# Two transformer blocks on one core: the convolution's sum and other intermediate values move from SBUF into PSUM

## The chip, the core and the metric

One core of a Trainium2 chip runs one program that computes everything: no host arithmetic, one launch. The metric is the device time of an execution in microseconds (us). In this program TensorE (PE) multiplies matrices out of SBUF into PSUM, of which each stage allots eight banks of 512 fp32 values per partition; VectorE (DVE) and ScalarE (ACT) work on both memories, GpSimd (POOL) on SBUF alone, and SyncE (SP) starts the DMAs.

## What is computed

The input is one sequence of 512 tokens of width 1024. A first block of two layers has three branches side by side: differential attention (two softmaxes per head, subtracted), bidirectional retention with a group norm, and grouped-query attention. Each branch is projected, multiplied by a sigmoid gate and summed:

```python
branches = jnp.stack([a, r, c], axis=2)
projected = jnp.einsum('bsnw,nwd->bsnd', branches, w_branch[l])
merged = jnp.sum(gates * projected, axis=2)
h = h + jnp.einsum('bsd,de->bse', merged, w_out[l])
```

Then an MLP with a squared ReLU. A second block of two layers has a 256-token context beside the sequence; its mixer concatenates a Fourier part, eight heads of latent attention (512 queries against 768 keys) and a convolution of 31 taps over 256 channels:

```python
def conformer_conv(zg, w_dw, b_dw, ln_g, ln_b, w_pw2):
    a, g = jnp.split(zg, 2, axis=-1)
    u = a * jax.nn.sigmoid(g)
    u = lax.conv_general_dilated(u, w_dw[:, None, :], ...,
                                 feature_group_count=CONV_WIDTH) + b_dw
    u = jax.nn.silu(layer_norm(u, ln_g, ln_b))
    return u @ w_pw2
```

In the first of these two layers the mixer runs for the sequence and the context, in the second for the sequence alone.

## The kernel before

Activations lie transposed, channels on partitions and tokens along the free axis. Every fp32 operand of a matmul is split into a high part (ACT copies it to fp32r, `hi`) and a low part (DVE subtracts it, `lo`), and three products stand for one. `out_split(y)` is this pair for an intermediate value: it reads `y` twice, once on ACT and once on DVE.

The program has eight stages, each with its own PSUM tags: for each layer a mixer and then a stage with output projection and MLP. The first block's mixers are `mixer1`, the second block's `mixer2`.

Nothing is issued as the code stands. Every operation is recorded (`Sched.record`), and at a stage's end `Sched.run` (line 283) places them: a list scheduler that takes, engine by engine, the ready operation of the lowest number, gives buffers from tags such as "mm" or "t" and holds an operation back while its tag is full. All instructions are issued by one line, so in the profile everything is L489 and only tile names tell groups apart: `cu` is the padded convolution input, `h`, `t`, `r`, `e`, `z`, `w` are SBUF tags, `mm`, `sc`, `acc` PSUM ones, and `sums` holds constant matrices. `_port` (line 532) lets DVE instructions with two SBUF operands and POOL instructions exclude each other in the scheduler's bookkeeping. Where PE would have nothing for a while, the scheduler puts in filler matmuls of `sums` with itself, whose result nobody reads. Engines work in the order that results, and semaphores between them are derived from the tiles that instructions touch.

Convolution (`taps`, line 1371, run by `conv`): for each stream and each half of the channels, 25 of the 31 taps are multiply-adds on DVE, with the sum in an SBUF tile `h`; the other 6 are products, in turn on ACT and POOL (`TAPS = 'AP'`), that POOL adds up in a second tile; POOL adds both at the end. The two channel halves are stepped together (`zip_longest`), and the steps are dealt out between the blocks of attention.

Latent attention (`attend`): for 128 queries, scores against 768 keys go into one of two slots of tag "sc2" (9 matmuls of 256 columns), DVE takes the minimum, ACT the exponential with its sum, PE transposes, ACT and DVE split, PE multiplies by the values. The two slots are two tiles of two banks each.

First block: `ret_attend` multiplies scores by a decay mask into SBUF, splits them, and normalises by head; `diff_attend` makes both exponentials in SBUF; `project` gates a branch and adds it to `merged` on POOL.

Of the kernel before, what the change touches and what calls it, by code (L numbers as in the profile page):

```python
# [12 lines left out]
F32 = mybir.dt.float32  # L13
# [6 lines left out]
P = 128  # L20
# [26 lines left out]
TICK = 3  # L47
# [4 lines left out]
B2 = {"sc2": 2, "mm tr acc ms": 4}  # L52
BESIDE = 6
TAPS = 'AP'
# [473 lines left out]
def _in_psum(x):  # L528
    return isinstance(x, View) and x.buf.tag in ("mm", "tr", "acc", "ms", "sc", "sc2")
# [36 lines left out]
def kernel(  # L566
# [195 lines left out]
    def normalized(y, rs, n):  # L762

        w, rt = t32(n), psum("tr", n)
        S.activation(w.rearrange("p (a b) -> p a b", b=64), rs.unsqueeze(2).to_broadcast([P, n // 64, 64]), AF.Copy)
        transposes(rt, w, n // P)
        V.tensor_tensor(out=y, in0=y, in1=rt, op=ALU.mult)
# [155 lines left out]
    def mixer1(l, mp, u):  # L923
# [137 lines left out]
        def project(n, bo, gated=False, early=[]):  # L1061

            for m in range(KB):
# [11 lines left out]
                V.scalar_tensor_tensor(out=g, in0=g, scalar=1.0, in1=pj, op0=ALU.add, op1=ALU.mult)  # L1075
                if not gated:
                    G.tensor_tensor(out=merged[m], in0=merged[m], in1=g, op=ALU.add)
                yield
# [13 lines left out]
        def diff_attend(hd, q, k, v, bo):  # L1092
            acc = psum("acc")
            for half in range(2):
                pt = [pair(T), pair(T)]
                for j in range(2):
                    es = [sc.alloc("e") for m in range(2)]
                    r0, r1 = (softmax(scores(q, k, m, half * 2 + j), es[m]) for m in range(2))
                    V.tensor_tensor(out=r1, in0=r1, in1=neglam, op=ALU.mult)
                    S.activation(es[0], es[0], AF.Copy, scale=r0)  # L1100
                    V.scalar_tensor_tensor(out=es[0], in0=es[1], scalar=r1, in1=es[0], op0=ALU.mult, op1=ALU.add)
                    to_pt(es[0], pt, j)
# [40 lines left out]
        def ret_attend(hd, q, k, v, z, bo):  # L1143
# [5 lines left out]
            for kt in range(4):  # L1149
# [13 lines left out]
            colsum(ms, ones128, squares(xc))  # L1163
            R = rstd(ms, 1e-5)
            r = t32()
            V.scalar_tensor_tensor(out=r, in0=xc, scalar=ncol(f"gn{l}", hd), in1=R, op0=ALU.mult, op1=ALU.mult)
            V.scalar_tensor_tensor(out=r, in0=r, scalar=0.5, in1=z, op0=ALU.mult, op1=ALU.mult)
            bo.append(out_split(r))
# [15 lines left out]
        def gqa_attend(i, q, k, v, out):  # L1184
# [16 lines left out]
            normalized(y, rs, T)  # L1201
            out.append(out_split(y))
# [80 lines left out]
        for m, _ in enumerate(project(0, bd, False, early)):  # L1283
            a, b = sc.alloc("r", pin=True), sc.alloc("r", pin=True)
            S.activation(a, merged[m], AF.Copy, scale=0.5)
# [743 lines left out]
```

## Time and profile before

| | us |
|---|---|
| median of 3 runs (3465.47 to 3468.73) | 3466.51 |
| the profiled execution | 3464.11 |
| its span, first to last instruction | 3462.3 |

| engine | busy us | share |
|---|---|---|
| PE | 3366.1 | 97% |
| DVE | 2293.6 | 66% |
| ACT | 1458.9 | 42% |
| POOL | 795.3 | 23% |

The shares are means over stages that differ. By the tiles used, the first block's mixers run from the start to 556 us and from 961 to 1493 us, the second block's from 1898 to 2196 us and from 2822 to 3047 us; projections and MLPs fill the rest. A matmul's busy time includes the filler.

### The profile page before, as it was taken

Reading aid. Unit: us, or ns where it says so; the run is one execution under the profiler, and the core shown is the slowest. Engines: PE = TensorE matmul, PEld = TensorE weight load, DVE = VectorE, ACT = ScalarE, POOL = GpSimd, SP = SyncE. Lnnn points to the kernel's source line nnn. Section 1 sums busy time; section 2 is a strip of 40 time slices with the busy share of each in tenths; the row PEclk is TensorE's granted clock in tenths of the full one; section 3 lists DMA queues with packets and bytes.
Section 4 is the critical chain, followed back from the end, with each engine's and each line's share of the span. In section 5 each row is a group of like instructions: output and inputs, shape, how many; then the busy total and the mean of one; then the engine's idle time right before and its main releaser. Section 6 shows DMA issues by size and latency. Waiting matters only on the chain.

```text
span 3462.3 us, 48309 instructions
## 1 busy us (share of the span) xinstructions
PE 3366.1 (97%) x18565; PEld 2901.3 (84%) x18565; DVE 2293.6 (66%) x4092; ACT 1458.9 (42%) x2751; POOL 795.3 (23%) x710
## 2 busy tenths in 40 slices
PE   8999999999999999999999988999999998999999
PEld 8888888888888888888888876898888887888888
DVE  8888875865388788658654998564443369963334
ACT  5555444322355554443223376441221244843223
POOL 3112323111131032231112443120110235320002
PEclk9999999999999999999999999999999999999999
DMA  3222223543332212236533110223332221123332
GB/s 126 64 71 67 74 67 134 191 168 127 106 101 65 71 61 80 73 134 195 176 128 116 46 37 7 98 80 112 109 109 92 68 81 48 32 79 98 97 96 81
DMA packets 100744, 326.14 MB, mean 94 GB/s; under 512 B 11168, under 2 KB 18336, under 8 KB 100512
## 3 DMA queue, kind: packets, MB, share of 16 engines
q1 hardware_dynamic: 100512, 323.05, 29.0%
q8 instruction: 145, 2.38, 0.3%
q14 instruction: 87, 0.71, 0.1%
HBM read 313.57 MB, written 9.44 MB: 93 GB/s over the span
## 4 chain that ended last, share of the span: by engine, by line
PE 84%; DVE 10%; ACT 3%; issue 2%; POOL 1%; DMA 0%; SPq 0%; DVEq 0%; ACTq 0%; POOLq 0%
PE mm L489 78%; PE sc L489 4%; DVE r L489 3%; DVE h L489 2%; DVE s L489 2%; PE acc L489 2%; DVE t L489 1%; ACT r L489 1%; DVE w L489 1%; ACT e L489 1%; ACT t L489 0%; DMA raw<-in_win_dram 0%; ACT w L489 0%; POOL t L489 0%; POOL x L489 0%
## 5 line engine op out<-in xcount | busy, mean ns | idle before, releaser
L489 PE MATMUL mm<-r,w 128*128 128x512 f32 (+2 forms) x12044 | 2521.2, 360 | 17.7 <-DVE w L489 7.5
L489 PEld LDWEIGHTS mm<-r,w 128*128 128x128 f32 (+1 forms) x12044 | 2009.0, 189 | 347.6 <-DVE w L489 11.0
L489 DVE TENSOR_TENSOR w<-raw,w 128x1024 fp32r<-128x1024 f32 (+2 forms) x466 | 588.2, 1270 | 639.6 <-issue 327.8
L489 ACT ACTIVATE w<-raw 128x1024 fp32r<-128x1024 f32 (+1 forms) x466 | 483.5, 1047 | 1035.1 <-PE mm L489 946.8
L489 ACT ACTIVATE e<-sc,s 128x512 f32<-128x512 f32 (+2 forms) x208 | 153.4, 740 | 99.6 <-DVE s L489 94.7
L489 POOL TENSOR_TENSOR x<-t,x 128x512 fp32r<-128x512 f32 (+1 forms) x58 | 83.0, 1434 | 409.1 <-ACT x L489 397.5
L489 PE MATMUL mm<-rc,w 128*128 128x256 f32 x768 | 166.1, 281 | 0.0
L489 PEld LDWEIGHTS mm<-rc,w 128*128 128x128 f32 x768 | 139.8, 189 | 20.2
L489 DVE TENSOR_REDUCE s<-sc 128x1 f32<-128x512 f32 (+2 forms) x208 | 151.4, 741 | 7.6 <-PE sc L489 7.1
L489 POOL TENSOR_TENSOR t<-t,t 128x512 f32<-128x512 f32 (+2 forms) x70 | 89.0, 1273 | 237.5 <-DVE t L489 200.3
L489 PE MATMUL mm<-r,r 128*128 128x256 f32 (+1 forms) x588 | 118.8, 333 | 8.1 <-DVE r L489 6.8
L489 ACT ACTIVATE t<-mm 128x512 f32<-128x512 f32 (+4 forms) x126 | 68.0, 540 | 135.0 <-PE mm L489 129.9
L489 DVE SCALAR_TENSOR_TENSOR h<-cu,half,h 128x512 f32<-128x512 f32 (+1 forms) x144 | 116.4, 819 | 0.5
L489 PE MATMUL mm<-sums 128*128 128x256 f32 x757 | 107.2, 291 | 9.7 <-DVE sums L489 6.4
L489 DVE TENSOR_TENSOR r<-mm,r 128x256 fp32r<-128x256 f32 (+1 forms) x266 | 105.6, 433 | 14.3 <-ACT r L489 12.4
L489 ACT ACTIVATE r<-mm 128x256 fp32r<-128x256 f32 (+1 forms) x272 | 94.8, 401 | 44.5 <-PE mm L489 41.3
L489 PEld LDWEIGHTS mm<-sums 128*128 128x128 f32 x757 | 101.2, 198 | 13.2 <-DVE sums L489 6.6
L489 ACT ACTIVATE r<-t 128x512 fp32r<-128x512 f32 (+3 forms) x141 | 83.1, 597 | 68.8 <-DVE t L489 55.9
L489 PEld LDWEIGHTS mm<-r,r 128*128 128x128 f32 x588 | 90.8, 193 | 23.4 <-DVE r L489 8.4
L489 DVE TENSOR_TENSOR r<-t,r 128x512 fp32r<-128x512 f32 (+2 forms) x134 | 105.4, 794 | 7.5 <-ACT r L489 6.3
L489 PE MATMUL mm<-w,r 128*128 128x256 f32 x704 | 102.4, 285 | 4.9 <-DVE w L489 3.1
L489 PEld LDWEIGHTS mm<-w,r 128*128 128x128 f32 x704 | 91.5, 190 | 7.4 <-DVE w L489 3.5
(636 smaller groups left out, 4358.8 us busy)
## 6 DMA issues: line engine op xcount, KB each, us to landing
raw<-in_wm_dram SPq DMA_DIRECT2D x256, 512.0 KB, 3.5
raw<-in_win_dram SPq DMA_DIRECT2D x134, 512.0 KB, 3.6
mraw<-in_wmod_dram SPq DMA_DIRECT2D x64, 512.0 KB, 4.4
raw<-in_wmod_dram SPq DMA_DIRECT2D x32, 512.0 KB, 3.5
raw<-in_wbr_dram SPq DMA_DIRECT2D x24, 512.0 KB, 3.5
raw<-in_wout_dram SPq DMA_DIRECT2D x16, 512.0 KB, 4.0
raw<-in_wo_dram SPq DMA_DIRECT2D x16, 512.0 KB, 3.5
kept<-h SPq DMA_DIRECT2D x24, 256.0 KB, 3.2
```

What stands on the lines that cost most here:

```text
L489: getattr(self.engines[eng], name)(*[_real(x) for x in a], **{n: _real(x) for n, x in k.items()})
```

## The change

In the second block, the convolution's running sum becomes one PSUM bank of its own, tag "cv". There is one, so a sum has to be finished before the next begins: the channel halves are stepped one after the other, and `TICK` and the count of steps double to deal out the same taps. The bank is won by packing both score slots into one tile of three banks, with slots of 768 columns where they had 1024. The products of the other six taps are all ACT's, and the last addition is DVE's. `normalized` (the softmax division after attention) and `fold` (Fourier) leave their result in PSUM.

In the first block, retention's masked scores and its group norm are computed in place in PSUM, and the ACT copy ahead of the group norm goes; differential attention's second exponential overwrites its scores; and for the last branch projected (n == 0) gate and sum are computed in the projection's own bank, on DVE, and split from there.

```diff
-TICK = 3
+TICK = 6
-B2 = {"sc2": 2, "mm tr acc ms": 4}
+B2 = {"sc2": 2, "mm tr acc ms": 4, "cv": 1}
-TAPS = 'AP'
+TAPS = "A"
...
 def normalized(y, rs, n):
-        V.tensor_tensor(out=y, in0=y, in1=rt, op=ALU.mult)
+        V.tensor_tensor(out=rt, in0=y, in1=rt, op=ALU.mult)
+        return rt
...
 def project(n, bo, gated=False, early=[]):
-                V.scalar_tensor_tensor(out=g, in0=g, scalar=1.0, in1=pj, op0=ALU.add, op1=ALU.mult)
-                if not gated:
+                V.scalar_tensor_tensor(out=g if n else pj, in0=g, scalar=1.0, in1=pj, op0=ALU.add, op1=ALU.mult)
+                if n == 0:
+                    V.tensor_tensor(out=pj, in0=merged[m], in1=pj, op=ALU.add)
+                elif not gated:
                     G.tensor_tensor(out=merged[m], in0=merged[m], in1=g, op=ALU.add)
-                yield
+                yield pj
...
 def diff_attend(hd, q, k, v, bo):
-                    es = [sc.alloc("e") for m in range(2)]
-                    r0, r1 = (softmax(scores(q, k, m, half * 2 + j), es[m]) for m in range(2))
+                    e, p0 = sc.alloc("e"), scores(q, k, 0, half * 2 + j)
+                    r0 = softmax(p0, e)
+                    p1 = scores(q, k, 1, half * 2 + j)
+                    r1 = softmax(p1, p1)
...
-                    V.scalar_tensor_tensor(out=es[0], in0=es[1], scalar=r1, in1=es[0], op0=ALU.mult, op1=ALU.add)
+                    V.scalar_tensor_tensor(out=e, in0=p1, scalar=r1, in1=e, op0=ALU.mult, op1=ALU.add)
...
 def ret_attend(hd, q, k, v, z, bo):
-                w = t32()
-                V.tensor_tensor(out=w, in0=ps, in1=dt[:, 384 - kt * P:896 - kt * P], op=ALU.mult)
-                wh, wl = out_split(w)
+                V.tensor_tensor(out=ps, in0=ps, in1=dt[:, 384 - kt * P:896 - kt * P], op=ALU.mult)
+                wh, wl = out_split(ps)
...
-            r = t32()
-            S.activation(r, acc, AF.Copy)
             xc = psum("ms")
-            colsum(xc, cen128, parts(r))
+            colsum(xc, cen128, parts(acc))
...
 for m, pj in enumerate(project(0, bd, False, early)):
-            S.activation(a, merged[m], AF.Copy, scale=0.5)
-            V.scalar_tensor_tensor(out=b, in0=merged[m], scalar=0.5, in1=a.bitcast(F32), op0=ALU.mult, op1=ALU.subtract)
+            S.activation(a, pj, AF.Copy, scale=0.5)
+            V.scalar_tensor_tensor(out=b, in0=pj, scalar=0.5, in1=a.bitcast(F32), op0=ALU.mult, op1=ALU.subtract)
...
 def taps(i, b):
-            a = accs[n, b] = sc.alloc("h", n)
-            c = sc.alloc("h", n)
+            a, c = psum("cv", n), sc.alloc("h", n)
...
-            G.tensor_tensor(out=a, in0=a, in1=c, op=ALU.add)
+            accs[n, b] = sc.alloc("h", n)
+            V.tensor_tensor(out=accs[n, b], in0=c, in1=a, op=ALU.add)
...
 def fold(ps):
-            f, y = t32(TC), t32()
+            f = t32(TC)
             S.activation(f, ps[:, TC:], AF.Copy)
-            V.tensor_tensor(out=y[:, :TC], in0=ps[:, :TC], in1=f, op=ALU.add)
-            V.tensor_tensor(out=y[:, TC:], in0=ps[:, :TC], in1=f, op=ALU.subtract)
-            return out_split(y)
+            V.tensor_tensor(out=ps[:, TC:], in0=ps[:, :TC], in1=f, op=ALU.subtract)
+            V.tensor_tensor(out=ps[:, :TC], in0=ps[:, :TC], in1=f, op=ALU.add)
+            return out_split(ps)
...
 def conv():
-            yield from zip_longest(block_taps(0), block_taps(1))
+            for b in range(2):
+                yield from block_taps(b)
...
 def phase(name, shares, slots=()):
                 if tag == "sc2":
-                    sc.slots(pp, tag, n, 1024, F32)
+                    t = pp.tile([P, n * 768], F32, tag=tag, name=tag)
+                    sc.tags[tag] = Tag([t[:, i * 768:(i + 1) * 768] for i in range(n)], 0)
```

Because the scheduler reads the new operands, the order changes on all engines of the four mixers. DVE at the convolution's beginning in the second block's second layer, before (`cu` the input, `h_143` and `h_144` the two channel halves' sums, `cu_22072` the second half's input):

```order
L489 SCALAR_TENSOR_TENSOR cu_22071<-t_122,mm_22065 128x512
L489 TENSOR_TENSOR w_107<-raw_108,w_107 128x8x32
L489 TENSOR_SCALAR h_143<-cu_22071,half,vec 128x512
L489 TENSOR_TENSOR w_103<-raw_109,w_102 128x1024
L489 SCALAR_TENSOR_TENSOR h_143<-cu_22071,half,h_143 128x512 x3
L489 SCALAR_TENSOR_TENSOR cu_22072<-t_121,mm_22063 128x512
L489 SCALAR_TENSOR_TENSOR h_143<-cu_22071,half,h_143 128x512
L489 TENSOR_SCALAR h_144<-cu_22072,half,vec 128x512
L489 SCALAR_TENSOR_TENSOR h_143<-cu_22071,half,h_143 128x512
L489 SCALAR_TENSOR_TENSOR h_144<-cu_22072,half,h_144 128x512
```

and changed, with `cv` the bank:

```order
L489 SCALAR_TENSOR_TENSOR cu_22083<-t_121,mm_22076 128x512
L489 TENSOR_TENSOR w_104<-raw_108,w_104 128x8x32
L489 TENSOR_SCALAR cv_22078<-cu_22083,half,vec 128x512
L489 TENSOR_TENSOR w_105<-raw_109,w_106 128x1024
L489 SCALAR_TENSOR_TENSOR cv_22078<-cu_22083,half,cv_22078 128x512 x6
L489 SCALAR_TENSOR_TENSOR cu_22084<-t_118,mm_22074 128x512
L489 SCALAR_TENSOR_TENSOR cv_22078<-cu_22083,half,cv_22078 128x512 x5
L489 TENSOR_TENSOR t_122<-t_122,mm_22075 32x512
L489 TENSOR_TENSOR w_104<-raw_110,w_107 128x1024
L489 TENSOR_TENSOR t_120<-t_120,mm_22076 32x256
```

The two halves' sums alternated; now a single sum advances in runs of up to six here and nine elsewhere, and eleven taps stand where five stood before the next step's work (`t_122`).

PE at a group of scores of the second block's second layer, with the semaphores that each instruction waits for; `sc_22061` and `sc_22062` are the two slots, before:

```order
L489 MATMUL sc_22061<-k0h,q0l 128x256
L489 MATMUL sc_22061<-k0h,q0h 128x256
L489 MATMUL sc_22061<-k0l,q0h 128x256
L489 MATMUL sc_22061<-k0h,q0l 128x256
L489 MATMUL mm_22063<-ident,e_22068 128x128 [waits DVE_49,Activation_49]
L489 MATMUL mm_22063<-ident,e_22068 128x128 x3
L489 MATMUL sc_22062<-k0h,q0h 128x256
L489 MATMUL sc_22062<-k0l,q0h 128x256
L489 MATMUL sc_22062<-k0h,q0l 128x256
```

and changed, where both slots are `sc_22073`:

```order
L489 MATMUL mm_22074<-ident,e_22082 128x128 x2
L489 MATMUL mm_22076<-ident,e_22080 128x128 [waits DVE_49,Activation_49]
L489 MATMUL mm_22076<-ident,e_22080 128x128 x3
L489 MATMUL sc_22073<-k0h,q0h 128x256 [waits DVE_49]
L489 MATMUL sc_22073<-k0l,q0h 128x256
L489 MATMUL sc_22073<-k0h,q0l 128x256
```

The group's first matmul waited for nothing that its engine had not already seen; now it waits for DVE. Of the 80 such groups in both layers, none waited for DVE before and 25 do now.

DVE at the end of the first block's first mixer, from the fifth output tile on (`z` a gate, `h` the sum of the other branches, `r` the split), before:

```order
L489 SCALAR_TENSOR_TENSOR z_188<-z_188,mm_166 128x512
L489 TENSOR_TENSOR w_105<-raw_110,w_103 128x1024
L489 SCALAR_TENSOR_TENSOR r_72<-h_141,r_83 128x512
L489 TENSOR_TENSOR w_104<-raw_108,w_106 128x1024
L489 TENSOR_TENSOR w_107<-raw_109,w_102 128x1024
L489 SCALAR_TENSOR_TENSOR z_183<-z_183,mm_165 128x512
L489 SCALAR_TENSOR_TENSOR r_82<-h_143,r_80 128x512
```

and changed:

```order
L489 SCALAR_TENSOR_TENSOR mm_165<-z_188,mm_165 128x512
L489 TENSOR_TENSOR mm_165<-h_141,mm_165 128x512
L489 SCALAR_TENSOR_TENSOR r_80<-mm_165,r_84 128x512
L489 TENSOR_TENSOR w_102<-raw_110,w_106 128x1024
L489 TENSOR_TENSOR w_103<-raw_108,w_107 128x1024
L489 TENSOR_TENSOR w_104<-raw_109,w_105 128x1024
L489 SCALAR_TENSOR_TENSOR mm_164<-z_184,mm_164 128x512
```

The addition that POOL made stands on DVE between gate and split, and the split reads the bank. Filler matmuls number 207, 111, 59 and 106 in the four mixers before, and 215, 119, 63 and 43 now.

## Rows read from the trace of the kernel before

**Rows 1.** Page, part 1: each engine's busy us, share of span, instructions.

```profile
PE 3366.1 (97%) x18565; PEld 2901.3 (84%) x18565; DVE 2293.6 (66%) x4092; ACT 1458.9 (42%) x2751; POOL 795.3 (23%) x710
```

**Rows 2.** Stretches, from:to and length, busy us (instructions) by engine, clock, DMA.

```profile
core 0: us, PE busy (x) PEld busy (x) DVE busy (x) ACT busy (x) POOL busy (x), PEclk, DMA share, GB/s
0.00:556.00 556.00, 540.88 (x2871) 457.35 (x2872) 443.25 (x871) 284.35 (x555) 135.81 (x105) 0.99 0.25 80
...
961.00:1493.00 532.00, 522.54 (x2774) 441.76 (x2773) 429.03 (x846) 271.95 (x529) 125.61 (x87) 1.00 0.25 77
...
1898.00:2196.00 298.00, 261.14 (x1723) 230.63 (x1723) 269.35 (x576) 182.79 (x433) 123.67 (x121) 0.96 0.13 42
...
2822.00:3047.00 225.00, 203.97 (x1360) 180.89 (x1359) 209.07 (x406) 140.90 (x314) 96.91 (x82) 0.98 0.15 49
```

**Rows 3.** DVE groups, 1898 to 2196 us: count, busy us, mean ns, idle before.

```profile
L489 DVE SCALAR_TENSOR_TENSOR h<-cu,half,h 128x512 f32<-128x512 f32 x48 | 44.3, 932 | 0.3
L489 DVE TENSOR_REDUCE s<-sc 128x1 f32<-128x768 f32 x32 | 30.1, 945 | 0.8 <-PE sc L489 0.8
L489 DVE SCALAR_TENSOR_TENSOR h<-cu,half,h 128x256 f32<-128x256 f32 x48 | 25.1, 541 | 0.1
```

**Rows 4.** DVE groups, 2822 to 3047 us: the convolution's.

```profile
L489 DVE SCALAR_TENSOR_TENSOR h<-cu,half,h 128x512 f32<-128x512 f32 x48 | 47.0, 986 | 0.2
```

**Rows 5.** Single instructions near 2854 us: start, us, engine, operation, [idle before].

```profile
2853.46 0.74 DVE L489 SCALAR_TENSOR_TENSOR h<-cu,half,h 128x512 f32<-128x512 f32 x1
...
2854.84 1.35 POOL L489 TENSOR_TENSOR h<-h,t 128x512 f32<-128x512 f32 x1
2854.97 1.78 DVE L489 SCALAR_TENSOR_TENSOR h<-cu,half,h 128x512 f32<-128x512 f32 x1
```

**Rows 6.** DVE groups of the whole run, nearest in kind.

```profile
L489 DVE TENSOR_TENSOR h<-h,mm 128x512 f32<-128x512 f32 x68 | 46.3, 681 | 11.0 <-PE mm L489 10.6
...
L489 DVE SCALAR_TENSOR_TENSOR z<-z,mm 128x512 f32<-128x512 f32 x40 | 27.1, 681 | 18.4 <-ACT z L489 10.8 <-PE mm L489 7.6
...
L489 DVE SCALAR_TENSOR_TENSOR h<-mm,mod1x,h 128x512 f32<-128x512 f32 x34 | 25.3, 745 | 5.6 <-PE mm L489 5.6
...
L489 DVE SCALAR_TENSOR_TENSOR hc<-mm,mod0c,hc 128x256 f32<-128x256 f32 x40 | 19.2, 480 | 32.5 <-PE mm L489 32.4
...
L489 DVE TENSOR_TENSOR t<-t,t 128x512 f32<-128x512 f32 x26 | 17.8, 686 | 0.6
...
L489 DVE TENSOR_TENSOR h<-h,mm 128x256 f32<-128x256 f32 x24 | 9.8, 417 | 11.6 <-PE mm L489 11.2
```

**Rows 7.** Chain of waits, 1898 to 2196 us, then 2822 to 3047: share by line.

```profile
by line: PE mm L489 29.4%; DVE r L489 11.4%; issue 11.0%; PE sc L489 6.7%; DVE h L489 6.7%; ACT r L489 5.8%; DVE s L489 5.3%; ACT e L489 5.3%; DVE t L489 3.9%; POOL t L489 2.9%; DVE w L489 2.1%; POOL x L489 2.0%; ACT t L489 1.8%; POOL h L48
...
by line: PE mm L489 29.7%; DVE r L489 10.9%; DVE h L489 8.1%; issue 7.8%; DVE s L489 6.7%; ACT r L489 5.5%; ACT e L489 5.1%; PE sc L489 4.8%; DVE t L489 3.1%; DVE w L489 2.9%; ACT t L489 2.3%; POOL x L489 1.7%; DVE k0h L489 1.2%; POOL h L48
```

**Rows 8.** ACT groups, 1898 to 2196 us: products of other taps.

```profile
L489 ACT ACTIVATE t<-cu,half 128x512 f32<-128x512 f32 x4 | 2.7, 711 | 0.0
L489 ACT ACTIVATE t<-cu,half 128x256 f32<-128x256 f32 x4 | 2.0, 505 | 0.0
```

**Rows 9.** Waits, 1898 to 2196 us: us in total, times, longest.

```profile
PE sc L489 <- ACT e L489: 7.1, 8, 1.8
...
DVE s L489 <- PE sc L489: 0.8, 1, 0.8
```

**Rows 10.** Single instructions at the end of the first mixer.

```profile
547.91 1.29 POOL L489 TENSOR_TENSOR h<-h,z 128x512 f32<-128x512 f32 x1 [6.61 <-DVE z L489]
549.24 0.63 ACT L489 ACTIVATE r<-h 128x512 fp32r<-128x512 f32 x1 [2.19 <-POOL h L489]
549.90 0.69 DVE L489 SCALAR_TENSOR_TENSOR r<-h,r 128x512 fp32r<-128x512 f32 x1 [2.13 <-ACT r L489]
```

**Rows 11.** PE group, 2822 to 3047 us: filler matmuls.

```profile
L489 PE MATMUL mm<-sums 128*128 128x256 f32 x109 | 15.1, 283 | 0.0
```

More of the change, by code (lines that the diff above doesn't have):

```diff
@@ L528, in _in_psum @@
 def _in_psum(x):
-    return isinstance(x, View) and x.buf.tag in ("mm", "tr", "acc", "ms", "sc", "sc2")
+    return isinstance(x, View) and x.buf.tag in ("mm", "tr", "acc", "ms", "sc", "sc2", "cv")
 def _port(eng, name, out, ins):
@@ L1096, in diff_attend @@
                 for j in range(2):
-                    es = [sc.alloc("e") for m in range(2)]
-                    r0, r1 = (softmax(scores(q, k, m, half * 2 + j), es[m]) for m in range(2))
+                    e, p0 = sc.alloc("e"), scores(q, k, 0, half * 2 + j)
+                    r0 = softmax(p0, e)
+                    p1 = scores(q, k, 1, half * 2 + j)
+                    r1 = softmax(p1, p1)
                     V.tensor_tensor(out=r1, in0=r1, in1=neglam, op=ALU.mult)
-                    S.activation(es[0], es[0], AF.Copy, scale=r0)
-                    V.scalar_tensor_tensor(out=es[0], in0=es[1], scalar=r1, in1=es[0], op0=ALU.mult, op1=ALU.add)
-                    to_pt(es[0], pt, j)
+                    S.activation(e, e, AF.Copy, scale=r0)
+                    V.scalar_tensor_tensor(out=e, in0=p1, scalar=r1, in1=e, op0=ALU.mult, op1=ALU.add)
+                    to_pt(e, pt, j)
                     if j:
@@ L1152, in ret_attend @@
                 mm3(ps, k[0][:, a], k[1][:, a], q[0], q[1], True, True)
-                w = t32()
-                V.tensor_tensor(out=w, in0=ps, in1=dt[:, 384 - kt * P:896 - kt * P], op=ALU.mult)
-                wh, wl = out_split(w)
+                V.tensor_tensor(out=ps, in0=ps, in1=dt[:, 384 - kt * P:896 - kt * P], op=ALU.mult)
+                wh, wl = out_split(ps)
                 mm3(acc, v[0][:, a], v[1][:, a], wh, wl, kt == 0, kt == 3)
                 yield
-            r = t32()
-            S.activation(r, acc, AF.Copy)
             xc = psum("ms")
-            colsum(xc, cen128, parts(r))
+            colsum(xc, cen128, parts(acc))
             ms = psum("acc2")
             colsum(ms, ones128, squares(xc))
+            V.scalar_tensor_tensor(out=xc, in0=xc, scalar=0.5, in1=z, op0=ALU.mult, op1=ALU.mult)
             R = rstd(ms, 1e-5)
[L1165 to L1168, printed above, removed]
+            V.scalar_tensor_tensor(out=xc, in0=xc, scalar=ncol(f"gn{l}", hd), in1=R, op0=ALU.mult, op1=ALU.mult)
+            bo.append(out_split(xc))
         def group_values():
@@ L1200, in gqa_attend @@
                 V.tensor_tensor(out=y[r], in0=y[r], in1=acc[r], op=ALU.add)
-            normalized(y, rs, T)
-            out.append(out_split(y))
+            out.append(out_split(normalized(y, rs, T)))
         got, bg, br, bd = {}, [], [], []
@@ L1282, in mixer1 @@
         mh, ml = [], []
-        for m, _ in enumerate(project(0, bd, False, early)):
+        for m, pj in enumerate(project(0, bd, False, early)):
             a, b = sc.alloc("r", pin=True), sc.alloc("r", pin=True)
-            S.activation(a, merged[m], AF.Copy, scale=0.5)
-            V.scalar_tensor_tensor(out=b, in0=merged[m], scalar=0.5, in1=a.bitcast(F32), op0=ALU.mult, op1=ALU.subtract)
+            S.activation(a, pj, AF.Copy, scale=0.5)
+            V.scalar_tensor_tensor(out=b, in0=pj, scalar=0.5, in1=a.bitcast(F32), op0=ALU.mult, op1=ALU.subtract)
             mh.append(a)
@@ L1722, in main @@
                 for si in range(len(both)):
-                    normalized(y[si], rs[si], both[si][2])
-                    split(*ya[si][i], y[si])
+                    split(*ya[si][i], normalized(y[si], rs[si], both[si][2]))
                 if i == 1:
@@ L1728, in mixer2 @@
         steps = main()
-        fills = [(fourier(ams), 4 if last else 6, FSTEP[l]), (cv, (31 - BESIDE + 4) * len(both) - ticks[0], CSTEP[l])]
+        fills = [(fourier(ams), 4 if last else 6, FSTEP[l]), (cv, (2 * (31 - BESIDE) + 4) * len(both) - ticks[0], CSTEP[l])]
         done = [0, 0]
```

## The prediction

> **What bounds the kernel now.** I read the page's busy times first, then the stretches of the program, then the groups of VectorE (DVE) instructions in the two stretches that hold the convolution, then single instructions there, the waits and the chain.
>
> TensorE (PE) is busy for 97% of the span [rows 1], so nothing that is done to other engines can pay more than what PE still loses. The stretches show where that is [rows 2]. The first block's mixers (0 to 556 us and 961 to 1493 us) keep PE busy for 540.9 of 556 and 522.5 of 532 us. In the second block's mixers it is 261.1 of 298 and 204.0 of 225 us, so PE is idle for 37 and 21 us, while DVE is busy for 269.4 and 209.1 us, 90% and 93%. There the reader is to see a DVE that is hardly ever free and a PE that waits in small pieces. The MLPs and output projections between them are left as they are, so the change is decided in those 523 us, and in the tails of the first block's mixers.
>
> In the two stretches the convolution is DVE's largest item of 512 columns: 48 multiply-adds of 512 columns at 932 ns and 48 of 256 at 541 ns in the first, 48 of 512 at 986 ns in the second [rows 3, 4]. Single instructions show why these means are high [rows 5]: one that GpSimd (POOL) joined late took 0.74 us, the next 1.78 us, begun just after a POOL addition of 1.35 us, as if it first had to see that one out. These instructions read two SBUF operands (the padded input and the sum) while POOL reads SBUF too.
>
> **The sum.** It is made against the profiled execution, 3464.1 us (span 3462.3), which lies 2.4 us under the median of the timed runs; those 2.4 us are added at the end.
>
> *Convolution's sum in PSUM.* The multiply-add keeps its count and shape, but then reads one SBUF and one PSUM operand and writes PSUM. No DVE instruction of before writes PSUM. The nearest rows with a PSUM operand are 681 ns (scalar a constant) and 745 ns (scalar a column, as here) for 512 columns, and 480 ns for 256 [rows 6]. I take 745 and 480; the ends are 681 ns and the 932 to 986 ns of today. First stretch: 48 x (932 - 745) = 9.0 us and 48 x (541 - 480) = 2.9 us; second: 48 x (986 - 745) = 11.6 us. The last addition of each sum moves from POOL to DVE: 2 x 681 and 2 x 417 ns (2.2 us) in the first stretch, 1.4 us in the second. DVE is relieved by 9.7 and 10.2 us, about 20.
>
> [...]
>
> How much of the 20 us reaches the end? Lower bound by the chain [rows 7]: the lines of DVE h, nearly all the convolution's, hold 6.7% of 298 us and 8.1% of 225 us on it, 20.0 and 18.2 us; shortened by their own 17% (11.9 of 69.4 us) and 25% (11.6 of 47.0 us) that is 8 us. Upper bound: all 20 us, since DVE works in order at 90 to 93%, and what isn't on the chain stands in the queue ahead of something that is. I take the upper end: the chain's other DVE lines, the splits and the score reductions, wait behind these instructions.
>
> *Products of the other taps.* Three of the six products of each sum go from POOL to ScalarE (ACT): 6 of 512 and 6 of 256 columns in the first stretch, 6 x 711 + 6 x 505 ns = 7.3 us, and 4.3 us in the second [rows 8]. ACT is busy for 182.8 of 298 and 140.9 of 225 us [rows 2], which covers it: 0, with 7.3 and 4.3 us as the price if the cover were gone. POOL's queue loses these and the last additions; it is idle half the time, and its gain counts only as fewer collisions, which is in the 745 ns.
>
> *Score slots.* The two score slots of the second block become columns 0 to 767 and 768 to 1535 of one tile. In the order of the changed program, 25 of the 80 groups of score matmuls wait for DVE, before none; what they wait for is the minimum over the other slot's scores, 945 ns for 768 columns [rows 3], although the columns are different ones. PE works in order, so the transposes and value products behind it wait too, and DVE waits for their results. Bounds: 0, if all falls in PE's 37 and 21 idle us; 25 x 0.945 = 23.6 us, if every wait starts with the reduction and is passed on. The row nearest is today's wait of PE for a slot, 7.1 us in 8 pieces, beside 0.8 us that DVE waited for scores [rows 9]: waits of PE for slots are mostly not passed on, since scores are made ahead. I take +5 us.
>
> *First block.* Retention's scores, group norm and the second softmax of differential attention stay in PSUM; one copy per retention head goes; no DMA is added or moved past a queue. All of it lies under a PE that is 97 to 98% busy there: 0. In the tail, the last branch's sum moves from POOL (1.29 us) to DVE (0.68 us) ahead of the ACT copy and the DVE split [rows 10]: 0.6 us less per layer at the end of the chain. Against it, DVE has three instructions per output tile where it had two, with a PSUM bank held through all of them, and the changed order has 8 more filler matmuls per layer, 0.14 us each (15.1 us for 109) [rows 11]: up to 1.1 us. Both together 0, bounds -1.2 and +2.2 us.
>
> *In place in the second block.* The products and folds written into PSUM cost one row's price either way (681 and 417 ns); their splits then read one SBUF operand less. Both under 1 us: 0.
>
> Sum: -20 + 5 = -15 us, so 3449 us by the profile, and 3451 us as the median.
>
> **The rivals.**
> *All of it opens up.* DVE is the wall in those 523 us, and when it is shorter PE's idle goes with it. For it: 90 to 93% busy. Against: the chain there is 36% PE by its own lines (29.4 + 6.7) [rows 7]. With the whole 20 us, no price for the slots and a third of PE's 58 idle us (19 us): 3464 - 39 = 3425, so 3427 us.
>
> *The write eats it.* An instruction that reads its predecessor's sum from PSUM and writes it back could cost as much as today's mean; in the changed order up to nine of one sum follow each other directly, where mostly two sums took turns. For it: no row of a DVE write to PSUM. Against: 745 ns with a PSUM read, and a chain of small dependent instructions isn't the same thing. Then -20 becomes between -5 and +3 (the moved additions cost 3.6 us, and collisions still fall a little), the slots +5: 3464 to 3472 by the profile, and with -2 for the sum 3469 us as the median. [...]
>
> *The shared slots decide: slower.* The place is the score pipeline of both second-block mixers. PE waits for DVE 25 times (up to 23.6 us); and in the changed order 34 of the 80 exponentials wait for matmuls that write the other slot, 9 of 0.14 us each, 1.25 us, up to 42 us. At half of both it is 33 us, and the end is 3464 - 20 + 33 = 3477, so 3479 us. It turns slower from 20 us on, 0.25 us per group. For it: the waits stand in the order. Against: DVE waited 0.8 us for scores in 298 us, so there is slack to use up first.
>
> [...]
>
> **How the numbers follow.** Forecast 0.42, all of it 0.20, the write 0.18, the slots 0.20. No change means within 0.2%, 7 us, about what a measurement of this kernel can tell: 3459.6 to 3473.4. The first two cases are faster (0.62), the third is the same (0.18), the fourth slower (0.20). The range leaves out half of the second case and half of the fourth: 3426 to 3478 us. The forecast's own range, with 12 to 20 us of the transfer and 0 to 5 for the slots, is 3446 to 3460 us.
>
> **What would show it.** Right: the multiply-adds at 720 to 770 ns with few over 1 us, DVE's busy time in both second-block mixers down by about 10 us each, both stretches shorter by some 7 us each, the others within 2 us. The slots: PE's waits for DVE's reductions, before none, with a sum under 10 us; over 20 us, or exponentials that wait for score matmuls, and the fourth case holds. The write: multiply-adds at 850 ns or more with POOL idle. I am wrong if the first block's mixers move by more than 3 us, since I give them nothing, or if the multiply-adds fall as said and the stretches don't.

## The result and the profile after

The changed kernel takes 3506.8 us (median of 4 runs, 3504.7 to 3513.0), the kernel before beside it 3466.0 us (4 runs). The ratio is 1.0121 with a 95% interval of 1.0104 to 1.0139: 41 us slower where 15 us less were forecast. Medians here and below leave out one execution of a later kernel (the order alone), which took 4147.3 us where its other ten took 3469.0 to 3475.3. The profiled execution took 3504.7 us, its span is 3503.0 us. Its page, part 1, answers to [rows 1]:

```profile
PE 3368.5 (96%) x18522; PEld 2896.0 (83%) x18522; DVE 2273.5 (65%) x4114; ACT 1463.3 (42%) x2761; POOL 737.4 (21%) x670
```

DVE and POOL do less, PE as much as before. The stretches tell where the time is, set against [rows 2] (columns as there; the ends are where the next stage's first matmul stands):

```profile
0.00:562.40 562.40, 542.77 (x2878) 458.93 (x2878) 441.45 (x880) 283.37 (x552) 123.76 (x97) 0.99 0.25 79
968.00:1506.00 538.00, 523.84 (x2777) 442.05 (x2777) 429.81 (x855) 270.08 (x525) 112.43 (x79) 1.00 0.24 76
1912.00:2219.00 307.00, 259.79 (x1723) 227.71 (x1723) 258.39 (x579) 188.24 (x446) 106.56 (x105) 0.98 0.12 41
2847.00:3087.00 240.00, 201.06 (x1291) 173.78 (x1289) 200.97 (x408) 145.37 (x319) 80.58 (x74) 0.97 0.14 45
```

All four mixers are longer: by 6.7 and 7.0 us in the first block, by 9.8 and 16.3 us in the second, measured between the first matmuls of neighbouring stages. The projections and MLPs kept their lengths within 1 us. In the second block DVE is busy for 11 and 8 us less, close to the 10 forecast for each, but the stretches grew. The groups of DVE there, first for 1912 to 2219 us (answering to [rows 3]), then for 2847 to 3087 us ([rows 4]):

```profile
L489 DVE SCALAR_TENSOR_TENSOR cv<-cu,half,cv 128x512 f32<-128x512 f32 x48 | 35.9, 748 | 0.7
L489 DVE TENSOR_REDUCE s<-sc 128x1 f32<-128x768 f32 x32 | 30.3, 952 | 14.7 <-ACT e L489 12.0 <-PE sc L489 2.4
L489 DVE SCALAR_TENSOR_TENSOR cv<-cu,half,cv 128x256 f32<-128x256 f32 x48 | 23.2, 482 | 0.8
```

```profile
L489 DVE SCALAR_TENSOR_TENSOR cv<-cu,half,cv 128x512 f32<-128x512 f32 x48 | 35.8, 745 | 0.4
L489 DVE TENSOR_REDUCE s<-sc 128x1 f32<-128x768 f32 x32 | 30.2, 954 | 17.6 <-PE sc L489 10.9 <-ACT e L489 6.5
```

The multiply-adds fell to 748, 482 and 745 ns in the mean; 745 and 480 were forecast. In the kernel before, the medians for 512 columns were already 748 and 744 ns: its means of 932 and 986 come from 26 of the 96 that took over 1 us, all of them begun while POOL was busy. Now none takes over 0.76 us. So the PSUM operand doesn't make an instruction faster, it takes away the long ones. The reductions, before which DVE had idled for 0.8 us in all, now have 14.7 and 17.6 us of idle time ahead of them. The waits of 1912 to 2219 us say of what (columns of [rows 9]):

```profile
DVE s L489 <- ACT e L489: 17.4, 22, 1.7
ACT e L489 <- PE sc L489: 15.3, 17, 2.1
PE sc L489 <- DVE s L489: 12.4, 15, 1.9
...
PE sc L489 <- ACT e L489: 8.4, 11, 1.3
...
DVE s L489 <- PE sc L489: 6.6, 8, 1.7
```

Three engines wait for one another in a ring. The third and second are the waits that the prediction counted (PE for the other slot's reduction, an exponential for the other slot's matmuls). The first is one it had not seen: DVE's reduction waits for ACT's exponential, and both only read scores. Of its 17.4 us, 12.3 stand before reductions; the other 5.1 stand before reciprocals, which need the exponential's sum and had 0.4 us before. In the order of the changed program 29 of the 80 reductions of the second block wait for ACT, before none.

### The profile page after: what moved, and what is told of

The parts are those of the page before. It is cut to its first block, busy times and chain, and to the rows that moved or that the text cites. A ratio compares the mean times of both kernels' runs of the same rounds, so it can differ in the third digit from the quotient of the medians.

```text
span 3503.0 us, 48206 instructions
## 1 busy us (share of the span) xinstructions
PE 3368.5 (96%) x18522; PEld 2896.0 (83%) x18522; DVE 2273.5 (65%) x4114; ACT 1463.3 (42%) x2761; POOL 737.4 (21%) x670
## 5 line engine op out<-in xcount | busy, mean ns | idle before, releaser
L489 ACT ACTIVATE r<-mm 128x256 fp32r<-128x256 f32 (+1 forms) x345 | 133.5, 433 | 113.8 <-DVE mm L489 72.3
L489 ACT ACTIVATE e<-sc,s 128x512 f32<-128x512 f32 (+1 forms) x176 | 131.1, 747 | 112.0 <-DVE s L489 87.2
L489 DVE TENSOR_TENSOR r<-mm,r 128x256 fp32r<-128x256 f32 (+1 forms) x324 | 139.6, 463 | 15.2 <-ACT r L489 12.7
L489 PE MATMUL mm<-sums 128*128 128x256 f32 x682 | 97.1, 291 | 7.0 <-DVE sums L489 6.1
L489 PEld LDWEIGHTS mm<-sums 128*128 128x128 f32 x682 | 91.7, 199 | 9.4 <-DVE sums L489 6.3
L489 DVE SCALAR_TENSOR_TENSOR cv<-cu,half,cv 128x512 f32<-128x512 f32 (+1 forms) x144 | 94.8, 658 | 1.9
L489 POOL TENSOR_TENSOR t2x<-t0x 128x512 f32<-128x512 f32 x28 | 33.6, 1202 | 249.5 <-ACT t0x L489 249.5
L489 POOL TENSOR_TENSOR t1x<-t3x 128x512 f32<-128x512 f32 x28 | 33.3, 1188 | 249.7 <-ACT t3x L489 245.8
```

The costliest lines, as they stand in the source:

```text
L489: getattr(self.engines[eng], name)(*[_real(x) for x in a], **{n: _real(x) for n, x in k.items()})
```

## The experiments

The theory: (a) two slots in one tile are guarded as one buffer, so that a write of one waits for every reader of the other and the readers wait in turn, and this loses more than the convolution gains; (b) in the first block a PSUM bank that is held longer stops PE. The rivals: the convolution's sum in PSUM or its new order, the products moved to ACT, a shared bank as such, and for the first block the other edits there. Times are medians; the kernel before beside each set took 3464.6 to 3465.4 us. A mixer's length in what follows is taken from the profile, from its first matmul to the end of its last (the idle time ahead of the next stage, up to 1.7 us, is left out); before they are 553.7, 531.1, 296.8 and 223.8 us. It is one execution each: kernels that leave a mixer's code as it was have 553.1 to 555.8, 531.1 to 535.9, 295.4 to 299.5 and 223.7 to 224.0 us, so a difference of a few us says little in the first three.

**The slots alone.**

```
-                    sc.slots(pp, tag, n, 1024, F32)
+                    t = pp.tile([P, n * 768], F32, tag=tag, name=tag)
+                    sc.tags[tag] = Tag([t[:, i * 768:(i + 1) * 768] for i in range(n)], 0)
```

> The kernel before, with one edit: the two score slots of the second block's mixers become columns 0 to 767 and 768 to 1535 of one tile. Nothing is left out. Theory (the shared tile makes PE's writes of one slot wait for DVE's and ACT's reads of the other): the changed kernel lost 9.8 and 16.3 us in the two second-block mixers although DVE's busy time there fell by 11 and 8 us, so the slots alone should cost at least those 26 us, and up to 45 us if the convolution's shorter instructions were passed on in full: 3492 to 3511 us; the first block's mixers unchanged within 1 us; DVE's waits for score matmuls (0.8 us before in the first of the stretches) and for exponentials appear as in the changed kernel. Rival 1 (the convolution's sum in PSUM, one sum after the other, makes the loss): within 7 us of before. Rival 2 (the products of the other taps on ScalarE delay the exponentials): within 7 us of before.

Measured: 3507.6 us, ratio 1.0120 [1.0107, 1.0134], 42.8 us more. This one edit costs as much as the whole change. Every engine has the same instructions in the same order as before, fillers included; what differs is where the slots lie (the next run settles that) and the waits between engines. The waits of the changed kernel are there, columns as in [rows 9] (the first of the second block's mixers; before, DVE waited there 0.8 us for score matmuls and 0.4 for exponentials):

```profile
DVE s L489 <- ACT e L489: 11.8, 12, 2.4
...
PE sc L489 <- ACT e L489: 11.1, 13, 2.3
DVE s L489 <- PE sc L489: 9.8, 12, 1.5
...
PE sc L489 <- DVE s L489: 6.6, 10, 1.3
```

The second block's mixers are 322.2 and 239.4 us long, 25.4 and 15.6 us more. The stretches of this kernel, three pieces of 25 us of the first mixer among them:

```profile
1900.00:2223.00 323.00, 273.34 (x1722) 238.74 (x1720) 270.43 (x576) 183.66 (x434) 122.03 (x121) 0.93 0.12 38
2075.00:2100.00 25.00, 16.89 (x122) 15.30 (x123) 18.92 (x50) 16.38 (x43) 4.27 (x4) 0.93 0.00 0
2100.00:2125.00 25.00, 20.73 (x117) 17.75 (x115) 19.07 (x46) 13.91 (x36) 12.78 (x18) 0.79 0.00 1
2150.00:2175.00 25.00, 18.20 (x94) 15.85 (x92) 15.86 (x37) 11.61 (x29) 7.36 (x10) 0.70 0.00 1
2850.00:3090.00 240.00, 206.50 (x1356) 180.75 (x1357) 210.12 (x406) 141.16 (x312) 96.08 (x82) 0.98 0.14 45
```

and the piece of the kernel before with its lowest clock there:

```profile
2123.00:2148.00 25.00, 19.62 (x120) 17.13 (x118) 19.33 (x47) 14.94 (x39) 7.28 (x9) 0.80 0.00 1
```

In the second mixer the loss is waits almost alone: the clock is 0.98 as before, and PE is busy for 2.5 us more. In the first, the granted clock has a mean of 0.93 where it was 0.96, and two pieces are at 0.79 and 0.70 (means over 25 us; inside the piece of the kernel before, the window of 1 us from 2130 us stands at 1.00, the one from 2140 us at 0.50). PE is busy there for 12 us more (261.1 to 273.3) with the same matmuls. So of the 25.4 us about half go with a slower PE; whether the waits brought the clock down was not tested apart.

**The same tile, but no bank with columns of both slots.**

```
+                    t = pp.tile([P, n * 1024], F32, tag=tag, name=tag)
+                    sc.tags[tag] = Tag([t[:, i * 1024:(i + 1) * 1024] for i in range(n)], 0)
```

> The kernel before with the two score slots as columns 0 to 767 and 1024 to 1791 of one tile of four banks, so that no bank holds columns of both slots. The waits in its order are the same as with the slots packed at 768. Nothing is left out. Theory (the waits follow the tile, and the waits make the loss): as with the packed slots, 3507 us within 4 us, with the same waits of VectorE for exponentials and scores. Rival (two engines in the shared middle bank disturb each other, which the packed slots pay beside the waits): 10 us or more below the packed slots, under 3498 us.

Measured: 3506.0 us, 1.0118 [1.0104, 1.0132], with mixers of 322.2 and 239.2 us and the same fall of the clock. The shared bank adds nothing that can be seen. It is the tile that is guarded: the loss stays when no bank is shared (3506.0 us beside 3507.6).

**One slot instead of two.** `B2 = {"sc2": 1, ...}` in the kernel before.

> The kernel before with one score slot of 1024 columns in the second block instead of two. Nothing is left out. Theory (sharing one tile takes from the second slot most of its worth, since a group of scores can't be written while the other is read): at least as slow as the two slots in one tile, 3507 us, and not by much, 3505 to 3530 us. Rival (the two slots in one tile still overlap usefully, and the 42 us come from a few places): far slower, over 3540 us.

Measured: 3515.6 us, 1.0144 [1.0130, 1.0158], 50 us more than before; the mixers are 306.8 and 264.9 us long. A second slot in the same tile is worth 8 us, of 50 that a second tile is worth. In the first mixer the single slot is even 15 us better than two in one tile, and its clock is 0.97, not 0.93. A likely reason, not tested apart, is that the scheduler knows of a single slot and orders for it, while of the shared tile it doesn't know: it thinks the second slot free and puts the score matmuls early, where PE then stands with everything behind them. The orders agree with that: with the shared tile every engine's is the one of before, with a single slot they differ.

**The convolution's sum beside shared slots.** The slots as above, and

```
-            a = accs[n, b] = sc.alloc("h", n)
-            c = sc.alloc("h", n)
+            a, c = psum("cv", n), sc.alloc("h", n)
...
-            yield from zip_longest(block_taps(0), block_taps(1))
+            for b in range(2):
+                yield from block_taps(b)
```

> The kernel before with the score slots in one tile and the convolution's sum in a PSUM bank with its new order, the final additions on VectorE; the products of the other taps stay partly on GpSimd, and the first block is as before. Nothing is left out. Read against the kernel with the slots alone. Theory: multiply-adds of 512 columns at 745 ns where they took 932 and 986; 8 us (the chain's share) to 20 us (all) less than the slots alone, and 15 to 30 us above the kernel before, since the second block of the changed kernel lost 26 us: 3481 to 3496 us. Rival 1 (the sum in PSUM makes the loss): 20 us or more above the slots alone. Rival 2 (the products on ScalarE): within 7 us of the kernel before or below it, since these are left out.

Measured: 3495.5 us, 1.0089 [1.0075, 1.0102], 12 us less than with the slots alone. So the sum in PSUM isn't what loses, and that rival falls. But the gain is lopsided: 304.1 us in the first mixer (18 less than with the slots alone, with the clock back at 0.98), 243.1 in the second (4 more). So part of the 18 is likely the clock's.

**Its order alone**, in SBUF, with two score tiles:

> The kernel before with the convolution's new order alone: one sum after the other instead of in turns, the planner's step at 6 instead of 3, both sums in SBUF, two score tiles. Nothing is left out. In the changed convolution, read against the slots alone, the first second-block mixer gained 18 us and the second lost 4, though VectorE's busy time fell by 17 and 16 us. Theory (the gain is the PSUM operand's, the loss in the second mixer is of the slots and of where the sum's instructions fall): multiply-adds of 512 columns stay at 900 to 990 ns, first mixer within 3 us of before, second within 4 us. Rival 1 (the order makes part of the shorter instructions): under 850 ns. Rival 2 (the order makes the second mixer's loss): the second mixer 4 us or more longer, the first unchanged.

Measured: 3470.5 us, 1.0018 [1.0009, 1.0027], 5.1 us more; mixers 294.6 and 228.5 us. The 17 and 16 us of DVE's busy time in this expectation are off: by the traces they are 12.4 and 14.2 us. The multiply-adds of 512 columns, first and second mixer:

```profile
L489 DVE SCALAR_TENSOR_TENSOR h<-cu,half,h 128x512 f32<-128x512 f32 x48 | 46.4, 967 | 0.3
```

```profile
L489 DVE SCALAR_TENSOR_TENSOR h<-cu,half,h 128x512 f32<-128x512 f32 x48 | 46.9, 976 | 0.2
```

The shorter instructions come from the PSUM operand and not from the order, and the order costs the second mixer 4.7 us: the second rival's mark. It is a loss that the prediction's sum doesn't have.

**The sum in PSUM without a shared tile.** Two score tiles of two banks each, four banks for "mm" and one for the sum are nine, where each stage allots eight. So this was tried with one slot, two banks for the sums, in turns as before, against the kernel with one slot:

> The kernel with one score slot of 1024 columns, and with the convolution's sums in two PSUM banks, in turns as before, the final additions on VectorE. Nothing is left out. Read against the kernel with one slot: its second-block mixers took 306.8 and 264.9 us, 10 and 41 us more than before. Theory (the shorter multiply-adds are passed on in a stretch that VectorE bounds, and lost where it waits for scores): multiply-adds near 745 ns; the first mixer 6 to 12 us shorter, since it is still near VectorE's time, the second within 5 us, since it waits for the single slot: 3501 to 3511 us. Rival (the saving is passed on nowhere but where shared slots had made waits): both mixers within 3 us of the kernel with one slot, 3513 to 3519 us.

Measured: 3509.3 us, 1.0126 [1.0111, 1.0142], 6 us less than with one slot. First the stretches of the kernel with one slot, then of this one, and its multiply-adds in the first mixer:

```profile
1901.00:2208.00 307.00, 263.58 (x1737) 230.64 (x1736) 271.60 (x575) 183.76 (x431) 121.45 (x121) 0.97 0.13 43
2835.00:3100.00 265.00, 221.11 (x1443) 195.08 (x1443) 214.82 (x406) 142.60 (x311) 95.07 (x82) 0.95 0.13 42
```

```profile
1902.00:2210.00 308.00, 268.09 (x1773) 236.39 (x1771) 268.31 (x578) 183.51 (x432) 112.62 (x117) 0.97 0.13 42
2836.50:3094.00 257.50, 212.62 (x1383) 185.95 (x1383) 207.25 (x408) 143.52 (x312) 87.53 (x80) 0.97 0.13 42
```

```profile
L489 DVE SCALAR_TENSOR_TENSOR cv<-cu,half,cv 128x512 f32<-128x512 f32 x48 | 35.3, 746 | 0.6
```

The sum of time was as expected, its places were the reverse: the first mixer, where 6 to 12 us were expected, gained nothing (+1.3), the second gained 7.7, where within 5 was said. DVE's multiply-adds of the first mixer are 13 us shorter than with one slot (907 to 746 ns and 578 to 477 ns, 48 each), but DVE's busy time there fell by 3.3 us only: the final additions take 2, and other instructions with SBUF operands became longer, such as the 16 casts of queries, 8.5 us with one slot and 11.3 now. The end doesn't move.

**The first block's edits alone**, score slots and convolution as before:

> The kernel before with the edits of the first block's mixers alone: the last branch's sum, retention's scores and group norm, differential attention's second softmax, and the product with the normalizer in PSUM; score slots, convolution and folds as before. Nothing is left out. The changed kernel's first-block mixers were 6.7 and 7.0 us longer. Theory (PSUM banks held through more instructions make PE wait in the first block, independent of the second): +11 to +16 us, 3477 to 3482 us, all of it in the two first-block mixers. Rival (they are longer only through what the scheduler or the second block's other edits do to them, such as the filler matmuls): within 5 us of before.

Measured: 3475.8 us, 1.0031 [1.0020, 1.0043], 11 us more. It is an independent second loss. Then one edit at a time:

> The kernel before with the sum of the first block's last branch in its PSUM bank alone (VectorE adds the merged branches in the bank, ScalarE and VectorE split it from there). Nothing is left out. The four edits of the first block together cost 11 us. Theory (a bank held through three VectorE instructions and one of ScalarE instead of one stops the tail's matmuls): most of the 11 us, +6 to +10 us, 3471 to 3475 us, all in the last 60 us of both first-block mixers. Rival (the loss is in retention or in the second softmax): within 2 us, or 1.3 us faster.

```
-                V.scalar_tensor_tensor(out=g, in0=g, scalar=1.0, in1=pj, op0=ALU.add, op1=ALU.mult)
-                if not gated:
+                V.scalar_tensor_tensor(out=g if n else pj, in0=g, scalar=1.0, in1=pj, op0=ALU.add, op1=ALU.mult)
+                if n == 0:
+                    V.tensor_tensor(out=pj, in0=merged[m], in1=pj, op=ALU.add)
+                elif not gated:
```

Measured: 3474.8 us, 1.0029 [1.0018, 1.0041]: 9.8 us, nearly all of it. PE in the tail of the first mixer, first before, then with the sum in its bank (start, us, engine, operation, [idle before]):

```profile
511.85 11.40 PE L489 MATMUL mm<-r,w 128*128 128x512 f32 x48
...
553.53 2.07 PE L489 MATMUL mm<-sums 128*128 128x256 f32 x16
555.66 6.64 PE L489 MATMUL mm<-r,w 128*128 128x512 f32 x28
```

```profile
512.98 8.65 PE L489 MATMUL mm<-r,w 128*128 128x512 f32 x36
521.47 2.07 PE L489 MATMUL sc<-sums 128*128 128x256 f32 x16
524.97 0.50 PE L489 MATMUL mm<-r1x,w 128*128 128x512 f32 x1 [1.42 <-DVE r L489]
...
558.27 1.83 PE L489 MATMUL mm<-sums 128*128 128x256 f32 x14
561.54 6.63 PE L489 MATMUL mm<-r,w 128*128 128x512 f32 x28 [1.44 <-DVE r L489]
```

Before, PE went through the tail's beginning without a stop. Now it stops when the next output tile has no bank: 2.07 us of filler matmuls and 1.42 us of idle time, until `DVE r`, the low half of the split, gives the bank back. The same before the next stage's first matmul (the last two rows): 3.3 us of filler and idle time where it was 2.1 us. That is 3.5 + 1.2 us per layer, 9.4 us for two. DVE in that kernel shows why the bank comes back so late:

```profile
519.62 0.69 DVE L489 SCALAR_TENSOR_TENSOR mm<-z,mm 128x512 f32<-128x512 f32 x1 [0.82 <-PE mm L489]
520.22 1.22 DVE L489 TENSOR_TENSOR w<-raw,w 128x1024 fp32r<-128x1024 f32 x1
521.36 0.69 DVE L489 TENSOR_TENSOR mm<-h,mm 128x512 f32<-128x512 f32 x1
521.96 2.35 DVE L489 TENSOR_TENSOR w<-raw,w 128x1024 fp32r<-128x1024 f32 x2
524.23 0.69 DVE L489 SCALAR_TENSOR_TENSOR r<-mm,r 128x512 fp32r<-128x512 f32 x1
```

Between the first reader (519.6) and the last (524.9) of one bank stand three splits of weights, 3.6 us, in DVE's queue. With the old code the first reader was the only one.

> The kernel before with the first block's last sum on VectorE instead of GpSimd, but from SBUF into SBUF: the PSUM bank is free after the first VectorE instruction, as before, while VectorE has the same third instruction as with the sum in the bank. Nothing is left out. Theory (the held bank makes the 9.8 us: PE waits for the sum's last reader at the start of the tail, where it stands four banks ahead of VectorE, and again before the MLP's first matmul): within 3 us of before, rather up to 1.2 us faster, since 1.29 us of GpSimd become about 0.7 us twice in the two layers. Rival (the third VectorE instruction per output tile makes it): +6 to +10 us.

Measured: 3467.8 us, 1.0006 [0.9997, 1.0014]. The third DVE instruction without the held bank costs 2.5 us by the medians (the interval goes from 1 us less to 4.9 us more), not 9.8; the bank is the rest. At the tail's start PE has these two rows in place of the 3.5 us:

```profile
523.69 0.87 PE L489 MATMUL sc<-sums 128*128 128x256 f32 x6
525.04 0.50 PE L489 MATMUL mm<-r1x,w 128*128 128x512 f32 x1 [0.48 <-DVE z L489]
```

> The kernel before with retention's scores and group norm in place in PSUM alone. Nothing is left out. One ScalarE copy of 512 columns per head goes, and the product with the decay matrix writes the score bank, which the split then holds. Theory: 0 to +3 us, 3464 to 3468 us, since a bank is held for one VectorE, one ScalarE and one VectorE instruction longer while PE has other branches' matmuls. Rival (retention makes the loss): +6 to +11 us.

Measured: 3467.8 us, 1.0008 [0.9999, 1.0016]. Its own mixers are 0.4 and 0.8 us longer, so most of the 2.7 us is no more than the scatter of runs.

> The kernel before with differential attention's second softmax in place in its PSUM bank alone, the scores of the second map asked for after the first softmax. Nothing is left out. Theory: +1 to +4 us, 3466 to 3469 us: the bank of the second map's scores is held until the two maps are joined, over the exponential, the reciprocal, one product and the joining, while before it was free after the exponential. Rival (this makes the loss): +6 to +11 us.

Measured: 3464.9 us, 1.0001 [0.9992, 1.0010]: nothing, less than I expected.

**What remains without slots and convolution, and a kernel below both.**

> The changed kernel without its score slots in one tile and without the convolution's sum in PSUM (two score tiles, the sum in SBUF, in turns): what stays are the first block's edits, the products of the other taps on ScalarE, and the folds and the product with the normalizer in PSUM. Nothing is left out. Theory: the 13 us of the first block and no more, 3477 to 3482 us, within 4 us of the kernel with the first block's edits alone; the second block's mixers within 2 us of before each. Rival 2 (the products on ScalarE cost): over 8 us above the kernel with the first block's edits alone.

Measured: 3471.4 us, 1.0018 [1.0009, 1.0027], 4.4 us under the kernel with the first block's edits alone, a gain that I had not expected; rival 2 falls, since the products on ACT are in it. So the harmless edits were put together, without the sum of the last branch and without retention's:

> The kernel before with what has cost nothing so far: differential attention's second softmax in place, the product with the normalizer and the folds in PSUM, and the products of the other taps on ScalarE. The sum of the last branch, retention, the score slots and the convolution's sum are as before. Nothing is left out. Theory: the kernel with the first block's edits, the folds and the products together stood 4.4 us under the one with the first block's edits alone, and the second softmax cost 0: 3459 to 3464 us, 1 to 6 us under before. Rival (the 4.4 us were chance, medians of 6 and 11 runs that lie 3 us to either side): within 2 us of before.

Measured: 3459.2 us, ratio 0.9981 [0.9972, 0.9990], 6 us under the kernel before. Its second-block stretches:

```profile
1902.00:2195.00 293.00, 258.26 (x1706) 226.94 (x1705) 268.58 (x575) 189.03 (x445) 115.13 (x109) 0.97 0.13 42
2820.00:3041.00 221.00, 199.56 (x1338) 177.71 (x1336) 205.34 (x407) 144.09 (x320) 87.39 (x76) 0.98 0.15 49
```

Each is about 4 us shorter than before ([rows 2]), with POOL busy for 9 us less in each, and PE for some 3 to 4 us less: 31 fewer filler matmuls in the two. Which of the folds, the normalizer's product and the products on ACT gives this was not tried apart. The normalizer's product is also in the kernel with the first block's edits alone, where the second of these mixers is as before (223.6 us), so there the gain is the folds' or the products'. On top of it, one slot and the sums in PSUM in the first of these mixers alone:

> The kernel with the four edits that cost nothing (second softmax, normalizer's product, folds, products of the other taps on ScalarE; 3459 us), and in the first of the second block's mixers alone one score slot and the convolution's sums in two PSUM banks, in turns; the second of these mixers has two score tiles and the sums in SBUF. Nothing is left out. Theory: one slot cost 10 us there, the shorter multiply-adds give back 6 to 12: 3455 to 3464 us, that is within 5 us of the kernel without this edit. Rival (in the changed kernel the edit gained 18 us in this mixer beside shared slots, and it does here too): 3449 to 3453 us. Rival (none of it is passed on): 3467 to 3471 us.

Measured: 3476.4 us, 1.0031 [1.0020, 1.0043], worse than any of the three expected. That mixer is 309.5 us long, 17 more than without this edit, about what the kernel with one slot and the sums in PSUM has there (308.1). A single slot there takes the other edits' gain with it.

## Why the prediction was wrong

*Convolution's sum, its price: right.* DVE's write to PSUM has the price of the nearest row with a PSUM read, as taken (748, 482 and 745 ns in the mean, where 745 and 480 were taken), and the rival in which the write eats the gain is out: 748 and 745 ns with a PSUM source stand against medians of 748 and 744 ns with two SBUF operands. What the sum saved is the long instructions that began while POOL was busy.

*Convolution's sum, how much reaches the end: wrong.* "I take the upper end", all 20 us. The runs gave 12 us beside shared slots (partly the clock's), 6 us beside one slot, of which none in the first mixer, and a loss of 5.1 us for the new order alone. The chain's share that I had as the lower bound, 8 us, was nearer. DVE busy for 90% of a stretch did not make it the wall: PE, ACT and DVE wait for one another there (17.4, 15.3 and 12.4 us in the changed kernel's first of these mixers), and the reading that fits is that a shorter instruction on one leaves it waiting for the others. What the sum is worth beside two separate score tiles was not tried.

*Score slots: the step that failed.* "+5 us", since "waits of PE for slots are mostly not passed on, since scores are made ahead": it is +42.8 us. The row that I leaned on showed waits for a slot when another slot could still be filled. With one tile there is no other: the scores stand as early in PE's order as before, but wait there until the readers of the other slot are through. The slack was the very thing that the change took. And its upper bound, 23.6 us, counted only PE's waits. The rival with the shared slots had the mechanism, its place and two of its three waits; its 33 us are within 10 of what was measured. It lacked DVE's waits for ACT (reader after reader), and the slower clock of the first mixer. It should have been the forecast.

*First block: wrong.* "Both together 0", at worst 2.2 us. The text saw the bank "held through all" three instructions and priced it as eight fillers. The bank was to be priced by its time in DVE's in-order queue, from first to last reader, weights' splits between them included (5.3 us instead of 0.7), against the 11.4 us that the matmuls of four output tiles take on PE (the 48 from 511.85 us before). That is 9.8 of the 11 us. My mark for it, over 3 us, was met.

*In place elsewhere, and products on ACT: 0.* Nothing clear of the scatter was lost, as said (retention's 2.7 us have an interval that holds 0); together they gain 4 to 6 us, which I had put under 1 us.

The parts add up to 42.8 - 12.1 + 11.0 - 4.4 = 37.3 us of the 40.8 measured. The rest of 3.5 us is within what these medians can tell. That the order's 4.7 us in the second mixer are part of its 16.3 is likely, but it was seen without shared slots only.

## What to carry to other kernels

A buffer is what the dependence tracking takes for one: before two double-buffered slots are packed into one tile, count every pair of instructions that becomes ordered, readers after readers too, and compare with the kernel that has one slot, because that is nearly what was left here (3507.6 us with two slots in one tile, 3515.6 with one slot). Before an intermediate value stays in a PSUM bank, follow the bank from its first write to its last reader through each engine's queue, with what other work stands in between, and ask what PE does when it finds no bank. The idle time that a wait shows today is no bound for it when the change takes away the slack that keeps it small.

## What the runs showed of the hardware that was not expected

- DVE instructions that read and write the same PSUM bank at every step of a chain of 24 took 744 to 749 ns for 512 columns (means of 48), the same as those that only read PSUM (745 ns, [rows 6]) and as the median with both operands in SBUF (748 and 744 ns). What differs is the tail: of the 96 with both operands in SBUF, 26 took 1.0 to 1.8 us, all begun while POOL was busy; of the 96 with the sum in PSUM none took over 0.76 us. In the other order the means with both operands in SBUF stayed at 967 and 976 ns.
- A stretch with more waits can also have a lower clock: with two slots in one tile the granted clock in the first of the second block's mixers went to 0.79 and 0.70 in pieces of 25 us, where the lowest piece before had 0.80, and PE was busy 12 us longer with the same matmuls. In the changed kernel, with much the same waits, the mean stayed at 0.98. A piece in which PE was busy for 16.9 of 25 us stands ahead of the 0.79, but in the changed kernel one with 15.4 us was itself at 1.00 and had 0.86 behind it; what decides is open.
